# Cached memory keys turned in 32x32 squares on VectorE, their scores as 32x32 products on sixteen tiles of the array, and the pools laid out anew

## The chip, the cores and the metric

The kernel runs on one core of a Trainium2 chip. The time is device time in microseconds (us) of one launch; the time before is the median of 3 runs. The engines are named PE (TensorE matmuls; PEld is its weight load), DVE (VectorE), ACT (ScalarE), POOL (GpSimd) and SP (SyncE, which issues most of the DMAs). Each engine works through its own instructions in a fixed order, so an instruction that waits holds all that stand behind it on that engine.

## The reference

One layer of a hybrid decoder serves a prompt group of 512 rows and a sample group of 8 sequences with 4 new tokens each (32 rows), with the same weights, all in f32. The mixer (an mLSTM and a differential attention) comes first, cross-attention second, a ConvFFN last. The change lies in the cross-attention:

```python
def mem_attend(h, mk, mv, w_mq, w_mo):
    B, T, _ = h.shape
    q = (h @ w_mq).reshape(B, T, MEM_HEADS, MEM_HEAD_DIM)
    s = jnp.einsum('bqhd,bkhd->bhqk', q.astype(jnp.float32), mk.astype(jnp.float32)) * (MEM_HEAD_DIM ** -0.5)
    p = jax.nn.softmax(s, axis=-1)
    o = jnp.einsum('bhqk,bkhd->bqhd', p, mv.astype(jnp.float32)).reshape(B, T, D_MODEL)
    return o.astype(h.dtype) @ w_mo
...
yp, ... = layer(yp, pos_p, da_attend_prompt, ..., mk_p, mv_p, ...)        # keys and values from mem_prompt
ys, ... = layer(ys, pos_s, attend_s, ..., cache_mem_k[l], cache_mem_v[l], ...)
```

There are 4 heads of 256 and 256 memory tokens. The prompt attends to one memory whose keys and values the kernel computes itself. Each sample sequence attends to a memory of its own that is cached in DRAM: keys and values of 256 tokens x 1024 numbers each, 1 MB and 1 MB for one sequence, 8 MB and 8 MB in all.

## The kernel before

Rows lie on 128 partitions. A product of two f32 matrices is made of three with numbers of reduced mantissa (a high part and a rest, "split": ACT casts, DVE subtracts); a matmul whose operands stay f32 leaves two records in the trace (the samples' scores and value products are of this kind).

*Weights.* Class `Weights` holds a plan. A slot (`slot_tile`, pool `wp`, tag "W", `NSLOT` = 4 buffers) holds 512 KB of a weight matrix, split; a stage (`stage`, pool `stg`, 6 buffers of 4 KB a partition) takes what the DMA brings. `pump` emits the loads for as many slots as are free, `get` hands one out in turn and `free` gives it back.

*The cross-attention* is written in this order. `mem_v` computes the prompt memory's values; the prompt memory's own keys and values are read back from DRAM (`mk_d`, `mv_d`) and split into `mkT` and `mvN`. Then comes the query projection, called the q gemm below: `gemmB` over 8 column blocks m of `w_mq`, 48 matmuls each. The first four run with `half_first=True` (all blocks of one half of the columns before the other, L465), the others block by block (L477). `ev_q` splits each result into `qh` and `ql`, and copies the samples' 32 columns into `qs`.

*The samples' keys.* `mk_load(i)` brings half a sequence's keys into a stage (16 loads of 512 KB), tokens on partitions. `mk_turn(i)` turns it by eight PE transposes (L1416, PSUM tile `tpk`) and two copies, one on ACT and one on DVE (L1417), into `kT`, which uses a weight slot. `mk_scores(b)` multiplies one sequence (L1424, `ssc`): for each head two matmuls, 128 rows of contraction x 32 queries, all 32 sample rows against that sequence's 256 keys; `sample_exp` takes the maximum and the exponential from PSUM.

*The prompt's softmax* is a pipeline `prompt` of 8 steps, of which `next(prompt)` emits one: `ch_soft` (scores `sca`, maximum `cnm` on DVE, exponential `cp` on ACT, reciprocal `csu`, scaling of `cp` on DVE), `ch_turn` (transposes `cpt`, split into `pT`), `ch_out` (products `cpo` with the values, split into `oT`). `mv_load(b)` brings a sequence's values into two stages `wst`, or into a weight slot as `vt`, and `mv_out(b)` multiplies (`pso`). `ost` turns its result. Then the output projection with `w_mo` begins (L407 to L409, `mm<-wslot,oT`).

*What sets the order.* A list scheduler puts the instructions of each engine in an order, starting from the order in which they are written; `tc.issue_after(x)` keeps the instructions written under it behind x, `burst` holds a run of matmuls together. A tile of a pool can be written again only when all that read its buffer before are done. The order around the change:

```python
    for i in range(6):
        mk_load(i)
    for i, _ in enumerate(gemmB(hqT, [ev_q(m) for m in range(4, 8)])):
        if i % 4 == 3:
            for j in (i // 2 - 1, i // 2):
                mk_turn(j)
                mk_load(j + 6)
```

so that keys are loaded six halves ahead of their transposes. Then come one step of `prompt`, the scores of sequences 0 to 3, the transposes of sequences 4 to 7 with a step between, the first value loads, a step, the other scores, more value loads, and the rest of the steps.

## Time and profile before

| | |
|---|---|
| median of 3 runs | 960.0 us (959.2 to 962.14) |
| profiled execution | 957.37 us, its span 955.6 us, mean granted clock 0.994 |
| PE busy | 933.3 us, 6619 matmuls |
| DVE, ACT, POOL busy | 600.3, 387.7, 196.4 us |
| q gemm | starts at 381.78 us, last matmuls at 435.80 us |
| `w_mo` projection | starts at 491.42 us |
| PE records of L1416 (`tpk`) | 128, 16.5 us of busy time |
| PE records of L1424 (`ssc`) | 128, 7.9 us of busy time |

A line of a group reads: source line, engine, operation, output<-inputs by the program's names, tile rows*columns on PE, shape and count, then busy time, mean ns of one, and the idle time of the engine just before these instructions with what ended it. A line of a timeline begins with start and length in us. Matmuls overlap in the pipeline, so the distance of two starts is a better price than a length.

### The profile page before, as it was taken

What the parts mean: (1) busy time and instruction counts of PE and PEld (TensorE: products, weight loads), DVE (VectorE), ACT (ScalarE), POOL (GpSimd) and SP (SyncE); (2) the same over time, 40 slices, a digit from 0 to 9 for tenths busy, and PEclk for the clock granted to TensorE, in tenths of its full rate; (3) what the DMA queues carried; (4) which work ended last, traced back from release to release, by engine and by line L of the source; (5) the groups of instructions that cost most, each with busy time, mean ns of one, the idle gap of its engine ahead of it and who ended that gap; (6) DMA issues with size and microseconds to landing.
All of it is one profiled execution on the core that took longest, in us unless ns stands there. A gap on an engine that the chain in (4) does not pass through costs nothing. (4 is left out here: it accounts for less than half of the span.)

```text
span 955.6 us, 17087 instructions
## 1 busy us (share of the span) xinstructions
PE 933.3 (98%) x6619; PEld 810.2 (85%) x6619; DVE 600.3 (63%) x1129; ACT 387.7 (41%) x750; POOL 196.4 (21%) x383
## 2 busy tenths in 40 slices
PE   8999999999999999999999999999999999999995
PEld 5899787889766778998767799989988997999974
DVE  6745145565886448635654769727758676676767
ACT  5655134344676357635544523332212222222232
POOL 6610000115432216300000454001110110110114
PEclk9999999999999999999999999999999999999998
DMA  8950023344825539946954743063053313512023
GB/s 296 296 178 1 1 88 136 88 131 137 275 82 171 173 100 346 289 137 188 344 195 115 206 133 88 4 177 89 4 144 82 119 26 81 162 48 89 24 92 116
DMA packets 120674, 130.27 MB, mean 136 GB/s; under 512 B 8568, under 2 KB 86233, under 8 KB 120593
## 3 DMA queue, kind: packets, MB, share of 16 engines
q1 hardware_dynamic: 114408, 125.69, 42.3%
q10 hardware_dynamic: 6184, 3.48, 1.2%
q8 instruction: 52, 0.85, 0.4%
q14 instruction: 30, 0.24, 0.1%
HBM read 112.22 MB, written 16.93 MB: 135 GB/s over the span
## 5 line engine op out<-in xcount | busy, mean ns | idle before, releaser
L146 ACT CAST wslot<-wst 128x1024 fp32r<-128x1024 f32 x125 | 130.8, 1050 | 261.3 <-issue 73.5
L477 PE MATMUL mm<-fT,wslot 128*128 128x256 f32 x1872 | 235.9, 288 | 0.0
L477 PEld LDWEIGHTS mm<-fT,wslot 128*128 128x128 f32 x1872 | 234.4, 188 | 1.8 <-issue 0.8
L147 DVE TENSOR_TENSOR wslot<-wst,wslot 128x1024 fp32r<-128x1024 f32 x125 | 154.4, 1238 | 91.8 <-ACT wslot L146 91.4
L1689 PE MATMUL mm<-wslot,act 128*128 128x512 f32 (+1 forms) x180 | 70.2, 391 | 0.0
L1690 PE MATMUL mm<-wslot,act 128*128 128x512 f32 (+1 forms) x180 | 70.0, 392 | 0.0
L1688 PE MATMUL mm<-wslot,act 128*128 128x512 f32 (+1 forms) x180 | 69.3, 387 | 0.0
L1596 POOL COPY cvo<-u 128x2 f32<-128x2 f32 x43 | 11.0, 256 | 204.7 <-DVE u L1594 194.6
L407 PE MATMUL mm<-wslot,hT 128*128 128x512 f32 x128 | 51.6, 403 | 0.0
L477 PE MATMUL mm<-hT,wslot 128*128 128x256 f32 (+1 forms) x384 | 51.0, 289 | 0.0
L409 PE MATMUL mm<-wslot,hT 128*128 128x512 f32 x128 | 51.0, 400 | 0.0
L408 PE MATMUL mm<-wslot,hT 128*128 128x512 f32 x128 | 50.7, 396 | 0.0
L1591 DVE TENSOR_TENSOR u<-mm,rsb 128x256 f32<-128x256 f32 x43 | 18.2, 424 | 51.0 <-PE mm L477 50.0
L477 PEld LDWEIGHTS mm<-hT,wslot 128*128 128x128 f32 x384 | 49.2, 188 | 0.5 <-issue 0.2
L1688 PEld LDWEIGHTS mm<-wslot,act 128*128 128x128 f32 x180 | 34.3, 191 | 8.0 <-issue 0.4
L1690 PEld LDWEIGHTS mm<-wslot,act 128*128 128x128 f32 x180 | 33.8, 188 | 7.2 <-issue 0.4
L1689 PEld LDWEIGHTS mm<-wslot,act 128*128 128x128 f32 x180 | 33.8, 188 | 7.2
L1608 ACT ACTIVATE c<-c 128x560 f32<-128x560 f32 x21 | 14.1, 672 | 56.5 <-DVE c L1602 56.5
L1602 DVE SCALAR_TENSOR_TENSOR c<-u,cvT,c 128x560 f32<-128x560 f32 x43 | 34.3, 798 | 0.9
L1601 DVE SCALAR_TENSOR_TENSOR c<-u,cvT,c 128x560 f32<-128x560 f32 x43 | 34.1, 793 | 0.2
L1701 DVE TENSOR_TENSOR yp<-mm,yp 128x512 f32<-128x512 f32 (+1 forms) x41 | 27.2, 674 | 5.1 <-PE mm L1690 5.0
L409 PEld LDWEIGHTS mm<-wslot,hT 128*128 128x128 f32 x128 | 24.1, 188 | 5.1
(474 smaller groups left out, 1863.8 us busy)
## 6 DMA issues: line engine op xcount, KB each, us to landing
wst<-in_w_up_dram SPq DMA_DIRECT2D x42, 512.0 KB
wst<-in_w_in_dram SPq DMA_DIRECT2D x28, 512.0 KB
wst<-in_w_down_dram SPq DMA_DIRECT2D x20, 512.0 KB
wst<-in_cache_mem_k_dram SPq DMA_DIRECT2D x16, 512.0 KB
wst<-in_w_mk_dram SPq DMA_DIRECT2D x8, 512.0 KB
xb<-in_x_prompt_dram SPq DMA_DIRECT2D x8, 512.0 KB
wst<-in_cache_dk_dram SPq DMA_DIRECT2D x16, 256.0 KB
wst<-in_cache_dv_dram SPq DMA_DIRECT2D x16, 256.0 KB
```

Source lines behind the costliest of these rows:

```text
L146: nc.scalar.copy(out=hi, in_=src)
L147: (eng or nc.vector).tensor_tensor(out=lo, in0=src, in1=f32(hi), op=SUB)
L407: mm(ps[b], lhsT=xt.hi(k, c0, c0 + n), rhs=s[:, 0, kk, :], start=(k == 0), stop=False)
L408: mm(ps[b], lhsT=xt.hi(k, c0, c0 + n), rhs=s[:, 1, kk, :], start=False, stop=False)
L409: return mm(ps[b], lhsT=xt.lo(k, c0, c0 + n), rhs=s[:, 0, kk, :], start=False, stop=(k == nk - 1))
L477: mm(ps[i], lhsT=s[:, l, k, :], rhs=x(k, c0, c1), start=(k == 0 and j == 0), stop=(k == 7 and j == 2))
L1601: STT(out=c, in0=u[:, 1:EXT - 1], scalar=w[1], in1=c, op0=MUL, op1=ADD)
L1602: STT(out=c, in0=u[:, 0:EXT - 2], scalar=w[0], in1=c, op0=MUL, op1=ADD)
L1688: mm(ps, lhsT=t[:, 0, c0:c0 + P], rhs=s[:, 0, i % 2, cs], start=st, stop=False)
L1689: mm(ps, lhsT=t[:, 0, c0:c0 + P], rhs=s[:, 1, i % 2, cs], start=False, stop=False)
L1690: return mm(ps, lhsT=t[:, 1, c0:c0 + P], rhs=s[:, 0, i % 2, cs], start=False, stop=en)
L1701: VTT(out=y, in0=ps, in1=y, op=ADD)
```

## The change

- The samples' keys of four sequences come straight into one tile `kq` (32 KB a partition, pool "k" with one buffer). `mk_turn(b)` turns each half of a sequence in place with one DVE instruction that transposes every 32x32 square of 128x1024. `tpk`, its copies and `kT` go.
- `q_spread` copies `qs` into `qrep`, such that each group of 32 partitions holds what each other one holds; 16 copies per half, on POOL, ACT and DVE in turn.
- `mk_scores(g)` works on four sequences at once: 128 matmuls of 32 rows of contraction x 32 queries x 256 columns, over 4 row groups and 4 column groups of the array, into 4 PSUM banks; four copies put the sums in order, then one maximum and four exponentials.
- The pools of weights and stages can be closed and opened again at other places. For the q gemm there are 2 slots and 2 stages in place of 4 and 6; stages are 6 again behind it, slots 4 again behind the second scores. All of `w_mq` now goes through the block-by-block form.
- The reads of `mk_d` and `mv_d` move into the q gemm (`own_memory`), and so do the 24 small loads of `cr` for the convolution, which move from SP's queue to ACT's (`conv_rows`).

```diff
-    for m in range(8):
-        slotB(w_mq, [(P * m, P)])
...
+    closed("st")
+    closed("w")
+    opened("w", 2, "left")
+    opened("st", 2, "left")
+    opened("k", 1, "right")
+    W.nslots = 2
+    for m in range(8):
+        slotB(w_mq, [(P * m, P)])
+    W.pump()
...
+            nc.scalar.dma_start(out=cr[p0 + q0:p0 + q0 + m, o:o + n], in_=src[:, c0:c0 + n])
...
-    run(gemmB(hqT, [ev_q(m) for m in range(4)], half_first=True))
...
+    def mk_load(b):
+        if b % 4 == 0:
+            kts[b // 4] = lay["k"][1].tile([P, 4, 2, DM], F32, name="kq", tag="K")
         for c in range(2):
-            for h in range(H):
-                t = mm(ps[NS * h:NS * h + NS], lhsT=qs[:, 2 * h + c], rhs=kts[b][:, 2 * h + c, :], start=(c == 0), stop=(c == 1))
-        sample_exp(sall, b, ps, nm, su)
-        return t.ins
+            dma(out=kts[b // 4][:, b % 4, c], in_=I["cache_mem_k"][0, b, c * P:(c + 1) * P].rearrange("t h d -> t (h d)"))
+
+    def mk_turn(b):
+        for c in range(2):
+            k = kts[b // 4][:, b % 4, c]
+            nc.vector.transpose(k, k)
+
+    def q_spread(m0):
+        n = 0
+        for j in range(4):
+            for i in range(4):
+                e = (nc.gpsimd.tensor_copy, nc.scalar.copy, VCP)[n % 3]
+                n += 1
+                e(out=qrep[NS * i:NS * i + NS, m0:m0 + 4, j, :], in_=qs[NS * j:NS * j + NS, m0:m0 + 4, :])
+
+    def mk_scores(g):
+        ps = [mmp("ssc") for _ in range(4)]
+        kt = kts[g].rearrange("p b c (j r) -> p (b c) j r", r=NS)
+        t = None
+        for j in range(8):
+            for i in range(4):
+                r = slice(NS * i, NS * i + NS)
+                for h in range(H):
+                    with burst(t):
+                        t = mm(ps[i][NS * h:NS * h + NS, :256], lhsT=qrep[r, 2 * h + j // 4, j % 4, :], rhs=kt[r, :, 8 * h + j, :],
+                               start=(j == 0), stop=(j == 7)).ins
...
+    mk_load(0)
+    for i, _ in enumerate(gemmB(hqT, [ev_q(m) for m in range(8)])):
         if i % 4 == 3:
-            for j in (i // 2 - 1, i // 2):
-                mk_turn(j)
-                mk_load(j + 6)
+            m = i // 4
+            if m < 4:
+                if m < 3:
+
+                    with tc.issue_after(wdma[-1].ins):
+                        mk_load(m + 1)
+                own_memory(m)
+                conv_rows(2 * m)
+                conv_rows(2 * m + 1)
+            if 1 < m < 6:
+                mk_turn(m - 2)
+            if m % 4 == 3:
+                q_spread(m - 3)
+    closed("st")
+    closed("w")
+    opened("st", 6, "left")
...
+    mk_scores(0)
+    mv_load(0)
+    mv_load(1)
+    for b in range(4, NB):
+        mk_load(b)
+    mv_load(2)
     next(prompt)
+    for b in range(4, NB):
+        mk_turn(b)
+    for _ in range(3):
+        next(prompt)
+    mk_scores(1)
+    closed("k")
+    opened("w", NSLOT, "right")
```

What the scheduler makes of it on DVE, around the softmax of the prompt's first steps and the keys of sequences 4 to 7. Before (`kT<-tpk` copies turned keys out of PSUM, `cnm`, `csu`, `cp` and `pT` are the prompt's softmax):

```order
L1035 TENSOR_REDUCE snm<-ssc 128x1 x2
L1417 COPY kT<-tpk 128x4x128
L1370 TENSOR_REDUCE cnm<-sca 128x2
L147 TENSOR_TENSOR pT<-cpt,pT 128x256
L1417 COPY kT<-tpk 128x4x128
L1374 RECIPROCAL csu<-csu 128x2
L1376 TENSOR_SCALAR cp<-cp,csu 128x256
L1417 COPY kT<-tpk 128x4x128
L1376 TENSOR_SCALAR cp<-cp,csu 128x256
L147 TENSOR_TENSOR pT<-cpt,pT 128x256
```

and now, on DVE from the maximum of the first score group on:

```order
L1470 TENSOR_REDUCE snm<-cas 128x4
L1445 STREAM_TRANSPOSE kq<-kq 128x1024
L1399 TENSOR_REDUCE cnm<-sca 128x2
L1445 STREAM_TRANSPOSE kq<-kq 128x1024
L157 TENSOR_TENSOR pT<-cpt,pT 128x256
L1403 RECIPROCAL csu<-csu 128x2
L1445 STREAM_TRANSPOSE kq<-kq 128x1024
L1399 TENSOR_REDUCE cnm<-sca 128x2
L1405 TENSOR_SCALAR cp<-cp,csu 128x256 x2
L157 TENSOR_TENSOR pT<-cpt,pT 128x256
L1445 STREAM_TRANSPOSE kq<-kq 128x1024 x2
```

Where copies out of PSUM stood, transposes of the loaded tile stand, and the first is ahead of the softmax's maximum.

On SP's queue, the loads around the q gemm's end. Before (`cr` are the convolution's rows, `xb<-x_d` the residual rows read back):

```order
L1407 DMA wst<-in_cache_mem_k_dram 128x1024
L1510 DMA cr<-in_w_dw_dram 3x64
L1511 DMA cr<-in_b_dw_dram 1x64
L1509 DMA cr<-in_state_conv_dram 16x64
L1510 DMA cr<-in_w_dw_dram 3x64
L1511 DMA cr<-in_b_dw_dram 1x64
L1407 DMA wst<-in_cache_mem_k_dram 128x1024
L1119 DMA xb<-x_d_2549 32x1024
L1407 DMA wst<-in_cache_mem_k_dram 128x1024
L1436 DMA wst<-in_cache_mem_v_dram 128x1024 x6
L1436 DMA vt<-in_cache_mem_v_dram 128x1024 x8
```

and now, on SP's queue from the fourth block of the weights on:

```order
L266 DMA wst<-in_w_mq_dram 128x8x128
L1440 DMA kq<-in_cache_mem_k_dram 128x1024 x2
L1349 DMA wst<-mk_d 128x1024
L266 DMA wst<-in_w_mq_dram 128x8x128
L1440 DMA kq<-in_cache_mem_k_dram 128x1024 x2
L1353 DMA wst<-mv_d 128x1024
L266 DMA wst<-in_w_mq_dram 128x8x128
L1353 DMA wst<-mv_d 128x1024
L266 DMA wst<-in_w_mq_dram 128x8x128 x2
L1483 DMA wst<-in_cache_mem_v_dram 128x1024 x6
L1440 DMA kq<-in_cache_mem_k_dram 128x1024 x8
L1131 DMA xb<-x_d_2549 32x1024
```

The keys of sequences 4 to 7 stood ahead of all values, one by one; they now stand as a block of eight behind six loads of values, and weights, keys and the own memory take turns ahead of that.

On PE, at the second half of the scores. Before (`tpk` are the keys' transposes):

```order
L1367 MATMUL sca<-mkT,qh 128x256 x2
L1367 MATMUL sca<-mkT,ql 128x256
L1416 MATMUL tpk<-cpk,wst 128x128 x40
L1424 MATMUL ssc<-kT,qs 32x256 x32
L1385 MATMUL cpt<-cpk,cp 128x128 x4
```

and now, on PE:

```order
L1396 MATMUL sca<-mkT,qh 128x256 x2
L1396 MATMUL sca<-mkT,ql 128x256
L1426 MATMUL cpo<-pT,mvN 128x512 x10
L1464 MATMUL ssc<-kq,qrep 32x256 x128
L1414 MATMUL cpt<-cpk,cp 128x128 x4
```

The transposes, which needed no result of the softmax, are gone from between its steps; what is left there depends on DVE and ACT.

More of the change, by code (lines that the diff above doesn't have):

```diff
@@ L209, in stage @@
     def stage():
-        return stg.tile([P, 1024], F32, name="wst", tag="st")
+        return lay["st"][1].tile([P, 1024], F32, name="wst", tag="st")
     def slot_tile():
-        return wp.tile([P, 2, 1024], F32R, name="wslot", tag="W")
+        return lay["w"][1].tile([P, 2, 1024], F32R, name="wslot", tag="W")
     def split_w(sv, st, share):
@@ L243, in slotsA @@
             slotA(w, k, n0, share=share)
+    wdma = []
     def slotB(w, ranges, share=False, extra=False):
@@ L1400, in ch_out @@
             put(oT, h // 2, j, j + 1, 0, SEQ, po.unsqueeze(1))
-    kst, kts, vts = {}, {}, {}
-    def mk_load(i):
-        b, c = i // 2, i % 2
-        kst[i] = stage()
-        dma(out=kst[i], in_=I["cache_mem_k"][0, b, c * P:(c + 1) * P].rearrange("t h d -> t (h d)"))
-    def mk_turn(i):
-        b, c = i // 2, i % 2
-        if c == 0:
-            kts[b] = wp.tile([P, 8, 256], F32, name="kT", tag="W")
-        for q in range(2):
-            ps = at("tpk")
-            for j in range(4):
-                t = tr(ps[:, j * P:(j + 1) * P], kst[i][:, (4 * q + j) * P:(4 * q + j + 1) * P], ident)
-            (VCP if q else nc.scalar.copy)(out=kts[b][:, 4 * q:4 * q + 4, c * P:(c + 1) * P], in_=v2(ps, P))
-        return t.ins
@@ new lines, in mk_turn @@
+    def mk_turn(b):
[20 more added lines that the diff above has]
+                               start=(j == 0), stop=(j == 7)).ins
+        b4 = slice(4 * g, 4 * g + 4)
+        for i in range(4):
+            (VCP if i % 2 else nc.scalar.copy)(out=sall[:, b4, :].rearrange("p b (c i r) -> p b c i r", c=2, i=4)[:, :, :, i, :],
+                                               in_=ps[i][:, :256].rearrange("p (b c r) -> p b c r", c=2, r=NS))
+        VRED(out=nm[:, b4], in_=sall[:, b4, :], axis=AX.X, op=MAX, negate=True)
+        for b in range(4 * g, 4 * g + 4):
+            ACT(out=sall[:, b, :], in_=sall[:, b, :], func=AF.Exp, bias=nm[:, b:b + 1], accum_out=su[:, b:b + 1])
+        return t
```

71 lines of the change are left out of this document (28 added, 43 removed).

## The prediction

> **What bounds the kernel now.** I read the head of the page first, then the timeline of TensorE (PE) from the query projection (the q gemm) to the output projection, then the groups of VectorE (DVE), ScalarE (ACT), SyncE's queue (SP), and the table by stretches.
>
> ```profile
> span 955.6 us, 17087 instructions
> PE 933.3 (98%) x6619; PEld 810.2 (85%) x6619; DVE 600.3 (63%) x1129; ACT 387.7 (41%) x750; POOL 196.4 (21%) x383
> ```
>
> PE is busy 98% of the span; no other engine is near it. Work taken off PE should shorten the kernel, as long as PE doesn't begin to wait. This is the part that the change touches (start, length, line, out<-in, tile, count; a length holds the last matmul's tail, so I take pitches from start to start):
>
> ```profile
> 412.91 1.47 PE L1416 MATMUL tpk<-cpk,wst 128*128 128x128 f32 x12
> 414.13 2.51 PE L477 MATMUL mm<-hqT,wslot 128*128 128x256 f32 x18
> 416.48 0.60 PE L1416 MATMUL tpk<-cpk,wst 128*128 128x128 f32 x4
> 416.83 4.00 PE L477 MATMUL mm<-hqT,wslot 128*128 128x256 f32 x30
> 436.19 1.03 PE L1416 MATMUL tpk<-cpk,wst 128*128 128x128 f32 x8
> 437.41 0.48 PE L1367 MATMUL sca<-mkT,qh 128*128 128x256 f32 x2
> 439.00 1.05 PE L1424 MATMUL ssc<-kT,qs 128*32 128x256 f32 x10
> 439.99 0.65 PE L1416 MATMUL tpk<-cpk,wst 128*128 128x128 f32 x4
> 440.57 3.22 PE L1424 MATMUL ssc<-kT,qs 128*32 128x256 f32 x54
> 443.72 1.53 PE L1416 MATMUL tpk<-cpk,wst 128*128 128x128 f32 x12
> 445.01 0.48 PE L1367 MATMUL sca<-mkT,qh 128*128 128x256 f32 x2
> 449.68 5.09 PE L1416 MATMUL tpk<-cpk,wst 128*128 128x128 f32 x40
> 454.70 3.66 PE L1424 MATMUL ssc<-kT,qs 128*32 128x256 f32 x64
> 458.29 0.66 PE L1385 MATMUL cpt<-cpk,cp 128*128 128x128 f32 x4
> 489.94 0.44 PE L1497 MATMUL ost<-cpk,oS 128*128 128x128 f32 x2 [1.50 <-ACT oS L1494]
> 490.86 0.72 PE L1397 MATMUL cpo<-pT,mvN 128*128 128x512 f32 x2
> 491.42 0.39 PE L407 MATMUL mm<-wslot,oT 128*128 128x512 f32 x1
> ```
>
> One wait stands in it, 1.50 us before `ost`. The prompt's softmax (`sca`, `cpt`, `cpo`) is mixed with transposes and scores, so PE has independent work while DVE and ACT finish a softmax; the DMA has room at first and little later (columns: us, busy time of PE, PEld, DVE, ACT, POOL with counts, clock, DMA share, GB/s):
>
> ```profile
> 440.00:450.00 10.00, 10.00 (x114) 8.38 (x114) 6.55 (x17) 6.15 (x21) 0.00 (x0) 1.00 0.55 154
> 460.00:470.00 10.00, 10.00 (x75) 8.23 (x74) 7.05 (x19) 6.46 (x28) 0.00 (x0) 1.00 1.03 408
> 520.00:525.00 5.00, 5.00 (x31) 3.80 (x21) 2.79 (x6) 2.72 (x5) 0.00 (x0) 1.00 1.11 294
> ```
>
> **PE work removed.** A block of 16 transposes within the q gemm takes 1.22 us (412.91 to 414.13) and 0.35 (416.48 to 416.83). Three such blocks, 4.71 us, lie before 436.19. Behind that: 1.22 (436.19 to 437.41), 0.58, 1.29, the block of 40 with 5.02, and 12 among `sca` at about 0.1 each, 1.14. All transposes: 13.96. The scores take 0.99 + 3.15 + 3.59 = 7.73. Together 21.7 us.
>
> **PE work added.** 256 products of 32x32 tiles, each two records, so 512 records with 256 columns. The shape is not in the trace; the bounds are. 54 score records with a 128x32 tile take 3.15 us, 58 ns each, with four column tiles in turn; a tile is therefore held about 233 ns. If all sixteen tiles work side by side, a record costs 15 ns and all cost 7.5 us, the lower end. If a row of tiles excludes the others, the price is 58 ns, 30 us, the upper end. How fast small products can be issued at all shows here:
>
> ```profile
> 229.98 0.25 PE L958 MATMUL mlg<-nT,qT 128*32 128x8 f32 x8
> 230.06 1.93 PE L962 MATMUL mlsi<-wst,qzm 128*32 128x128 f32 x64
> ```
>
> Eight records left in 0.08 us, 10 ns each, and the 64 behind them at about 29 ns with tiles held half as long, so issue is not the limit at 15. I take 7.5, 3.75 per group of four sequences. The Trainium skill ("TensorE: Matmul & The Clock Gate", section "Wait — 56ns, not 53.3ns?") says that starts are never closer than about 25 ns; 512 of them would be 12.8 us, an estimate from that page, and 5.3 us more than the sum here. The 10 ns row speaks against it for separate tiles.
>
> If nothing waited, PE would gain 21.7 - 7.5 = 14.2 us, and the 1.50 before `ost` as well, since `ost` now stands behind output-projection matmuls: 15.7 us, or 944. The question is how much PE waits.
>
> **First wait: the q gemm's weights.** One column block m of it takes 6.1 us (2.51 and 4.00 less tails, 48 records). Before, four slots and six stages were filled ahead. Now there are two of each, and the stages also carry the memory's own keys and values. From m = 3 on, a weight load can be issued only when the split of the block before has freed its stage. Such a load, and the split:
>
> ```profile
> 518.35 11.16 SPq L254 DMA_DIRECT2D wst<-in_w_up_dram  x8
> 522.52 1.05 ACT L146 CAST wslot<-wst 128x1024 fp32r<-128x1024 f32 x1 [1.64 <-DMA wst<-in_w_up_dram]
> 523.60 1.23 DVE L147 TENSOR_TENSOR wslot<-wst,wslot 128x1024 fp32r<-128x1024 f32 x1 [2.15 <-ACT wslot L146]
> ```
>
> Issue to cast 4.17, cast 1.05, subtraction 1.23: 6.5 us against 6.1 for a block, and more where a 512 KB key transfer is ahead in the queue (1.3 us at 408 GB/s) or a transpose ahead on DVE. The chain has four such links and some 2 us of slack at its start. Ends: 0 (all in the slack) and 8 (two key transfers ahead in each link, less slack). I take 3. ACT also gets the 24 small conv loads, 0.3 us each by SP's row, 7 us in all; they can hold a cast when their issue waits, which is in the 3.
>
> ```profile
> 425.71 0.30 SPq L1510 DMA_DIRECT2D cr<-in_w_dw_dram  x1
> L1064 ACT COPY caz<-spt 128x32 f32<-128x32 f32 x8 | 0.8, 223 | 0.0
> L1417 ACT COPY kT<-tpk 128x512 f32<-128x512 f32 x16 | 9.4, 588 | 2.6 <-PE tpk L1416 2.4
> ```
>
> **The end of the q gemm**, called E, would be 436.19 - 4.71 = 431.5 without the wait. Behind it come 12 `sca` (437.41 to 439.00, 1.6 us); the spread of the queries, 16 copies on three engines behind the last evacuation, keeps the first score waiting about 1.3 us (five small copies of 0.22 us on an engine, and an evacuation); the scores end at E + 6.6.
>
> **Second wait: the second group's keys.** This is the heart of the forecast. There is one key tile for four sequences, so the second group's loads start only when the first group's last score is done. On SP's queue they stand behind six value loads, which wait for the end of the q gemm.
>
> ```profile
> wst<-in_cache_mem_k_dram SPq DMA_DIRECT2D x16, 512.0 KB
> 448.81 6.32 SPq L1436 DMA_DIRECT2D wst<-in_cache_mem_v_dram  x6
> 455.94 5.49 SPq L1436 DMA_DIRECT2D vt<-in_cache_mem_v_dram  x8
> ```
>
> At 408 GB/s each 512 KB needs 1.28 us. Six value loads fill the DMA to about E + 8.5; eight key loads land from E + 10.5 to E + 19.5. On DVE the eight transposes of this group stand in turn with the prompt's softmax, the first ahead of the softmax's next maximum. So the softmax waits for transfers too. The DVE work there, by rows:
>
> ```profile
> L147 DVE TENSOR_TENSOR wslot<-wst,wslot 128x1024 fp32r<-128x1024 f32 x8 | 9.7, 1223 | 11.1 <-ACT wslot L146 11.1
> L1417 DVE COPY kT<-tpk 128x512 f32<-128x512 f32 x16 | 11.0, 687 | 9.1 <-PE tpk L1416 9.1
> L1370 DVE TENSOR_REDUCE cnm<-sca 128x2 f32<-128x512 f32 x8 | 5.5, 690 | 3.7 <-PE sca L1367 3.6
> L147 DVE TENSOR_TENSOR pT<-cpt,pT 128x256 fp32r<-128x256 f32 x16 | 6.7, 421 | 4.1 <-ACT pT L146 3.9
> L1376 DVE TENSOR_SCALAR cp<-cp,csu 128x256 f32<-128x256 f32 x16 | 5.1, 350 | 0.2
> ```
>
> A transpose of 128x1024 isn't in the trace. The subtraction of that size (1223 ns) is nearest; two 128x512 copies from PSUM are 1374. Ends 1.1 and 2.4 (twice the subtraction); I take 1.2. Between the first and the last transpose stand three maxima (2.1), three `pT` (1.3), four scalings (1.4) and two reciprocals (0.3): with eight transposes 14.7 us from E + 10.5, so to E + 25, and two more `pT` and the `cpo` behind them bring the second scores to E + 27.5. PE's own work up to there is 1.6 + 1.3 + 3.75 and 48 `sca`, 12 `cpt`, 12 `cpo` (9.9 us at about 0.12, 0.1 and 0.23 each), 16.5. PE so waits about 11 us here, where it waited nothing. Ends: 4 (values and keys pass side by side and transposes at 1.1) and 20 (transposes at 2.4).
>
> **Behind the second scores** (3.75 us) the value tiles `vt` take the keys' place: eight loads, 10.3 us, against some 13 us of PE work ahead of the first `pso`; hidden. A last softmax that has lost its cover costs about 1 us (0 to 3).
>
> **At no cost:** 16 DVE and 16 ACT copies of keys go (11.0 us and 9.4 at 588 ns), both engines having room; the evacuation copies and one maximum per group replace eight maxima and lie beside PE work; the conv loads leave SP's queue.
>
> **Sum:** 15.7 gained, less 3 + 1.3 + 11 + 1 = 16.3 waited: 0.6 us slower. The profiled execution took 957.37 us (span 955.6 and 1.77 around it), so 958.0 there; against the median of 960.0, the same step gives 960.6, and I say 960.5. From no change a measurement here can tell about 0.3%, 2.9 us.
>
> **Rivals.** (a) The waits are short: q gemm fed in time, PE covering much of the key transfer. For it: PE has `sca` and `cpo` to do, and DVE and ACT are under 75% busy in all rows. Against it: the order on DVE puts each softmax step behind a transpose. With the low ends (0 + 1.3 + 4) the gain is 10.4, 949.6; with no wait at all 944.3. (b) The sixteen tiles don't run side by side, or issue binds at 25 to 29 ns: at 29 ns, 14.8 us of scores, 7.3 more, 968; the sign is decided from about 20 ns on. For it: no row here has four rows of tiles in use. Against it: the 10 ns row. If instead rows of tiles take turns, 30 us of scores and 983. By the Trainium skill's 25 ns it would be 966. (c) Transposes at 2.4 us: 8 x 1.2 more on DVE's chain, 970; decided from 1.6 us on. (d) The q gemm starves, 8 us in place of 3: 965.5; decided from 6. For it: 6.5 against 6.1 with nothing in front. That the products stay whole and the change does nothing can't be; the instructions are others.
>
> **Chances.** The case of the sum 0.47: its waits move it by some 4 us to either side (956 to 965), so of it 0.13 faster, 0.24 the same, 0.10 slower. (a) 0.23, nearly all faster. (b) 0.10 (issue 0.07, rows in turn 0.03), (c) 0.10 and (d) 0.10, slower but for 0.05 that other terms make up. So faster 0.36, same 0.29, slower 0.35. The range reaches from (a) with its low ends, less a little, to (b): 947 to 968.
>
> **What would show it.** Right: no `tpk` of keys, score records at about 15 ns from start to start, and PE idle about 11 us between the two score groups, released by DVE, whose own idle time is put down to the `kq` transfers. Wrong: score groups of over 5 us; transposes far from 1.2 us; PE idle in the q gemm by more than 5 us or not at all; or PE busy through the second group's load, which would leave the gain whole.

## The result: 1.4% slower

After the change the median is 972.55 us (968.41 to 975.15, 4 runs) against 959.6 of before on the same chip (957.26 to 962.14, 4 runs): 1.0136 times, interval 1.0113 to 1.016. The forecast was 960.5, with 947 to 968 as its range. The profiled execution has a span of 968.9 us; before it was 955.6. The head of the page after:

```profile
span 968.9 us, 17576 instructions
PE 933.1 (96%) x6875; PEld 804.3 (83%) x6875; DVE 612.9 (63%) x1137; ACT 383.6 (40%) x748; POOL 200.2 (21%) x395
```

PE is busy as long as before (933.3), though 21.7 us of its work went and the new products take less: other work came back as longer busy time (why, the last section says), and the span grew by waits. PE's timeline of after, where before had its list (start, length, line, out<-in, tile, count, and in brackets the idle time before a row and what ended it):

```profile
439.82 0.39 PE L1396 MATMUL sca<-mkT,qh 128*128 128x256 f32 x2
...
441.32 3.41 PE L1464 MATMUL ssc<-kq,qrep 32*32 32x256 f32 x116
445.36 1.46 PE L1464 MATMUL ssc<-kq,qrep 32*32 32x256 f32 x60 [0.63 <-DVE qrep L1453]
448.65 2.92 PE L1464 MATMUL ssc<-kq,qrep 32*32 32x256 f32 x80 [1.83 <-issue]
451.50 0.80 PE L1396 MATMUL sca<-mkT,qh 128*128 128x256 f32 x2
...
460.83 0.44 PE L1414 MATMUL cpt<-cpk,cp 128*128 128x128 f32 x1 [3.78 <-DVE cp L1405]
...
464.94 1.22 PE L1426 MATMUL cpo<-pT,mvN 128*128 128x512 f32 x2 [0.46 <-ACT pT L156]
...
468.05 0.50 PE L1396 MATMUL sca<-mkT,qh 128*128 128x256 f32 x2 [1.39 <-ACT cp L1402]
...
471.98 0.76 PE L1464 MATMUL ssc<-kq,qrep 32*32 32x256 f32 x24
473.16 4.28 PE L1464 MATMUL ssc<-kq,qrep 32*32 32x256 f32 x205 [0.42 <-DVE oT L157]
478.47 0.71 PE L1464 MATMUL ssc<-kq,qrep 32*32 32x256 f32 x27 [1.03 <-issue]
479.11 0.66 PE L1414 MATMUL cpt<-cpk,cp 128*128 128x128 f32 x4
...
505.60 0.50 PE L419 MATMUL mm<-wslot,oT 128*128 128x512 f32 x1
...
511.02 0.38 PE L1554 MATMUL ost<-cpk,oS 128*128 128x128 f32 x2
```

The transposes are gone, and `ost` no longer holds PE. But the score groups last from 441.32 to 451.50 and from 471.98 to 479.11, 10.18 and 7.14 us, where 3.75 each was forecast. Within them PE stands still for 0.63, 1.83, 0.42 and 1.03 us, twice with "issue" as the reason: nothing that the profile shows held it. Between them it stands still for 5.63 us (3.78, 0.46 and 1.39). From these starts the touched part divides into stretches (us; the q gemm from its first matmul; "first scores" from its end to the end of the first score group; "behind" up to the first output-projection matmul, where the forecast is what its sum leaves):

| | q gemm | first scores | between | second scores | behind |
|---|---|---|---|---|---|
| forecast | 52.7 | 6.65 | 20.9 | 3.75 | 26.2 |
| after | 57.06 | 11.68 | 20.48 | 7.14 | 26.48 |
| difference | +4.4 | +5.0 | -0.4 | +3.4 | +0.2 |

They add to 12.6 us; the profiled execution took 970.69, 12.7 more than the 958.0 forecast for it. So two terms failed, the projection's wait and the price of the score groups, and the large one, the wait between the groups, came out as forecast. That a size is right doesn't yet make its reason right.

### The profile page after: what moved, and what is told of

Its sections match the earlier page's. It is cut to its first block, busy times and chain, and to the rows that moved or that the text cites. A ratio compares the mean times of both kernels' runs of the same rounds, so it can differ in the third digit from the quotient of the medians.

```text
span 968.9 us, 17576 instructions
## 1 busy us (share of the span) xinstructions
PE 933.1 (96%) x6875; PEld 804.3 (83%) x6875; DVE 612.9 (63%) x1137; ACT 383.6 (40%) x748; POOL 200.2 (21%) x395
## 4 chain that ended last, share of the span: by engine, by line
PE 75%; DVE 9%; DMA 6%; ACT 4%; issue 2%; POOL 2%; SPq 0%; DVEq 0%; ACTq 0%; POOLq 0%
PE mm L489 31%; PE mm L419 5%; PE mm L420 5%; PE mm L421 5%; PE mm L477 4%; PE mm L1733 4%; PE mm L1731 4%; PE mm L1732 4%; DVE wslot L157 1%; DMA xb<-in_x_prompt_dram 1%; PE mm L398 1%; DVE xb L1146 1%; PE sda L1223 1%; DMA kq<-in_cache_mem_k_dram 1%; ACT wslot L156 1%
## 5 line engine op out<-in xcount | busy, mean ns | idle before, releaser
L489 PE MATMUL mm<-hqT,wslot 128*128 128x256 f32 (+1 forms) x384 | 51.6, 295 | 5.2 <-ACT wslot L156 4.2
L489 PEld LDWEIGHTS mm<-hqT,wslot 128*128 128x128 f32 x384 | 50.3, 194 | 6.2 <-ACT wslot L156 4.7
```

The costliest lines, as they stand in the source:

```text
L489: mm(ps[i], lhsT=s[:, l, k, :], rhs=x(k, c0, c1), start=(k == 0 and j == 0), stop=(k == 7 and j == 2))
```

## The experiments

All on the two theories that the table leaves. A: a 32x32 record costs more than 15 ns, and PE's pauses add to it. B: with two slots and two stages the projection starves; rival to B: it is the conv loads' issue on ACT's queue. For the wait between the groups: transfer or transposes. All were timed in turn with the kernel before, in groups on four chips, whose medians for the kernel before are 958.03 to 959.42, so ratios and stretches compare better than medians. Stretches as above (in e7 and e8 some of the prompt's `sca` stand ahead of the projection's last block and count in it); the q gemm starts at 382.4 to 386.3 us, which the edits don't set.

| | q gemm | first scores | between | second | median us | ratio to before, 95% |
|---|---|---|---|---|---|---|
| e1_conv_sp | 54.11 | 11.69 | 21.93 | 8.17 | 970.5 | 1.0113 (1.0096 to 1.013) |
| e2_reuse | 56.56 | 10.56 | 13.13 | 6.33 | 963.4 | 1.0043 (1.0024 to 1.0062) |
| e3_n128 | 58.52 | 10.68 | 18.83 | 5.99 | 969.43 | 1.0089 (1.0064 to 1.0113) |
| e4_keys_first | 58.28 | 8.70 | 20.18 | 6.68 | 969.56 | 1.0098 (1.0072 to 1.0125) |
| e5_conv_late_keys_first | 53.34 | 8.69 | 19.37 | 8.29 | 963.92 | 1.0062 (1.004 to 1.0084) |
| e6_reuse_conv_sp | 54.50 | 11.40 | 13.63 | 7.01 | 960.06 | 1.0024 (0.9998 to 1.005) |
| e7_turns_held | 55.35 | 10.36 | 17.36 | 10.07 | 967.4 | 1.0102 (1.0077 to 1.0126) |
| e8_half | 56.42 | 12.93 | 11.79 | 3.59 | 972.3 | 1.0144 (1.0118 to 1.0171) |
| e9_softmax_ahead | 53.50 | 8.70 | 23.69 | 7.32 | 967.5 | 1.0091 (1.0069 to 1.0112) |
| e10_one_j | 53.13 | 5.95 | 18.91 | 1.79 | 956.62 | 0.9973 (0.9956 to 0.999) |
| e11_rows_inner | 53.00 | 8.70 | 19.82 | 6.78 | 965.05 | 1.0059 (1.004 to 1.0078) |
| e12_turns_no_load | 52.73 | 11.15 | 18.41 | 7.17 | 965.45 | 1.0069 (1.0044 to 1.0093) |
| e13_no_keys | 59.14 | 12.28 | 13.64 | 6.65 | 966.72 | 1.0078 (1.0048 to 1.0108) |

### The projection: e1_conv_sp

In the timeline of after, ACT (ACTq: its DMA issues) shows a cast that waited:

```profile
386.88 0.38 ACT L1378 ACTIVATE qh<-mm 128x256 fp32r<-128x256 f32 x1
...
390.22 0.34 ACTq L1367 DMA_DIRECT2D cr<-in_state_conv_dram  x1
...
395.72 0.23 ACTq L1367 DMA_DIRECT2D cr<-in_b_dw_dram  x1
...
397.95 1.04 ACT L156 CAST wslot<-wst 128x1024 fp32r<-128x1024 f32 x1 [10.69 <-DMA cr<-in_w_dw_dram]
```

ACT did no arithmetic for 10.69 us: it stood in the conv loads' issue, and the next weights' cast stood behind them. On PE of after:

```profile
384.73 11.32 PE L489 MATMUL mm<-hqT,wslot 128*128 128x256 f32 x86
399.05 0.76 PE L489 MATMUL mm<-hqT,wslot 128*128 128x256 f32 x4 [3.00 <-ACT wslot L156]
...
420.89 0.76 PE L489 MATMUL mm<-hqT,wslot 128*128 128x256 f32 x4 [1.23 <-ACT wslot L156]
```

The edit sends these loads through SP, behind the projection:

```diff
-            nc.scalar.dma_start(out=cr[...], in_=src[...])
+            dma(out=cr[...], in_=src[...])
@@ in the projection's loop
-                conv_rows(2 * m)
-                conv_rows(2 * m + 1)
@@ behind it
+    for g in range(8):
+        conv_rows(g)
```

> The 24 small conv loads go back to SP's queue, behind the weights of the query projection, as before the change; nothing else differs. Theory A (the query projection starved because ACT stood behind conv loads that waited for landings: 10.7 us between two of ACT's instructions from 386.9 to 398.0 in the changed kernel): the waits of 3.0 and 0.5 us in front of the third block go, and the low clock behind them; the projection ends 4 to 6 us earlier and the kernel takes 966 to 969 against 972.6. Theory B (two slots and two stages starve it, whoever issues the conv loads): waits of about the same sum remain, at most 1 us is gained, 971 to 973.

The q gemm fell by 2.95 us to 54.11, and the cast that waited 10.69 us starts at 392.76, 5.2 us earlier. So the rival to B takes 3 of the 4.4 us that the projection is over its forecast; theory A had 4 to 6 us, theory B at most 1. What is left is mostly a wait on DVE's half of the split. In the timelines of e1_conv_sp, first PE's, then SP's:

```profile
399.19 12.45 PE L489 MATMUL mm<-hqT,wslot 128*128 128x256 f32 x96 [2.13 <-DVE wslot L157]
```

```profile
450.58 0.32 SPq L1367 DMA_DIRECT2D cr<-in_state_conv_dram  x1
451.63 3.96 SPq L1440 DMA_DIRECT2D kq<-in_cache_mem_k_dram  x8
```

Little of the gain reached the end (970.5, where theory A had 966 to 969): the conv loads now stood ahead of the second group's key loads on SP, which left at 451.63 though the first scores had ended at 449.02, and the wait between the groups grew by 1.45 us.

### The second group's keys taken away: e2_reuse, e6_reuse_conv_sp

```diff
-    for b in range(4, NB):
-        mk_load(b)
+    kts[1] = kts[0]
...
-    for b in range(4, NB):
-        mk_turn(b)
```

> The keys of sequences 4 to 7 are neither loaded nor turned; the second scores use the first group's keys, so those sequences' scores are not the reference's. Theory A (the wait for the second group's keys costs about what was forecast, 10 to 11 us between the two score groups): PE has 20.5 us there in the changed kernel and only 10 of work, so the stretch shrinks to 10 to 13 us and the kernel takes 962 to 965. Theory B (the softmax of the prompt itself is the bound there, now that no transposes of keys cover it): the stretch stays above 17 us and less than 4 us are gained, 969 to 972.

The stretch between the groups fell from 20.48 to 13.13 us, and the median by 9.1, theory A. It is the largest single term. The 13.13 that stay hold 9.9 us of PE work by the prediction's count; in e2's PE timeline they are 10.6 of work and two waits of the softmax itself:

```profile
455.46 0.30 PE L1414 MATMUL cpt<-cpk,cp 128*128 128x128 f32 x1 [2.09 <-DVE cp L1405]
...
457.97 0.73 PE L1426 MATMUL cpo<-pT,mvN 128*128 128x512 f32 x2 [0.46 <-ACT pT L156]
```

With both edits:

> Both at once: the second group's keys neither loaded nor turned (its scores use the first group's keys and are not the reference's), and the conv loads on SP's queue. Theory A (the two causes are independent; without the second wait the 2.7 us at the query projection reach the end): 960 to 961.5, 2 to 3.4 us under the run without the second keys. Theory B (ACT's queue behind the conv loads is worth nothing in the end): 963 to 964.

The median lies in theory A's range, but the two runs were on different chips. By the ratios e6 gains some 1.8 us over e2, with intervals that overlap, and in the profiled executions nothing: the four stretches add to 86.5 us in e6 and 86.6 in e2, since the three behind the projection took back its 2.1. That the two costs are independent is so not shown. Even without the second group's keys and with the projection's gain the kernel only meets the one before, 1.0024.

### The records' price: e3_n128, e11_rows_inner, e10_one_j

e3_n128 leaves the products' number and shortens them to half the columns:

```diff
-  ...mm(ps[i][NS*h:NS*h+NS, :256], ..., rhs=kt[r, :, 8*h+j, :],
+  ...mm(ps[i][NS*h:NS*h+NS, :128], ..., rhs=kt[r, 0:4, 8*h+j, :],
```

> Score products over 128 columns in place of 256 (half of the keys; the other half of the scores is a copy of the first), with the same number of matmuls and weight loads; the evacuation has eight smaller copies per group in place of four. Theory A (a score record is priced by what PE has to issue and fetch, not by the array): the second group's records stay near 20 ns from start to start and its 7.1 us at 6.5 to 7.5, pauses of over 1 us included; the kernel takes 971 to 973. Theory B (the array's tiles are the bound, 14.6 ns at 256 columns): the pitch falls to about 8 ns, the second group to 3 to 4 us, the kernel to 965 to 968.

Its second score group in PE's timeline:

```profile
474.78 2.90 PE L1464 MATMUL ssc<-kq,qrep 32*32 32x128 f32 x205 [0.95 <-DVE oT L157]
478.92 0.50 PE L1464 MATMUL ssc<-kq,qrep 32*32 32x128 f32 x27 [1.24 <-issue]
```

A row's length ends with its last record's own, 0.29 us here and 0.37 with 256 columns. The starts of the 205 records so lie within 2.61 us, 12.8 ns apart, against 3.91, 19.1 ns, with 256 columns: neither theory A's 20 nor theory B's 8, and the time, 969.43, is between the two as well. Half the columns saves 6.4 ns, so a record of 256 is some 12.7 ns of columns, near the 15 taken, and 6.4 that don't go with the columns. Times sixteen tiles that is about 103 ns for each use of a tile. The weight loads of after have that length (count, then least, median and longest ns; the records' own lengths in after and then in e3 below):

```profile
L1464 PEld LDWEIGHTS ssc<-kq,qrep x512: 101/104/172, 441.3 to 478.6; 32*32 32x32 f32 x171
L1464 PE MATMUL ssc<-kq,qrep x512: 371/396/629, 441.3 to 478.8; 32*32 32x256 f32 x171
```

```profile
L1464 PE MATMUL ssc<-kq,qrep x512: 264/290/418, 445.4 to 479.2; 32*32 32x128 f32 x171
```

So a tile seems to be held for its load (104) and its columns (about 203), and the forecast took the columns alone. The fixed share is measured; that it is the load is an inference from equal lengths. The starts in the traces leave it open: they come in batches of 34 records, most of them 16 to 17 ns apart in after, with a gap of about 160 ns behind each batch (42 to 45 in e3), where two rounds of sixteen tiles would be 32.

The Trainium skill ("TensorE: Matmul & The Clock Gate", Part 3, section "The mechanism") says that a weight load overlaps running matmuls only if its row group differs. In the kernel four products in a row, eight records, share theirs. e11_rows_inner, built on e5, changes the row group with each product:

```diff
-            for i in range(4):
-                r = slice(NS * i, NS * i + NS)
-                for h in range(H):
+            for h in range(H):
+                for i in range(4):
+                    r = slice(NS * i, NS * i + NS)
```

> As the run with late conv loads and keys first, with the loops of the score products exchanged: the four row groups of the array inside, the four column groups (heads) outside. Theory A (a pass holds its tile for the matmul and its weight load, 216 + about 125 ns, whatever the order): pitch 20 to 22 ns, 963 to 965. Theory B (the order keeps weight loads from going ahead): 15 to 17 ns, 1 to 2 us less per group, 960 to 962.

Its PE timeline:

```profile
467.68 4.84 PE L1464 MATMUL ssc<-kq,qrep 32*32 32x256 f32 x226 [0.39 <-DVE oT L157]
472.81 0.70 PE L1464 MATMUL ssc<-kq,qrep 32*32 32x256 f32 x26 [0.29 <-issue]
```

The starts lie within 4.84 - 0.37 = 4.47 us, 19.9 ns a record: no gain, theory A. A batch of 34 takes 647 ns in both orders, so the order of the tiles is not what keeps the fixed share visible. The Trainium skill's floor of about 25 ns between starts (the same title, section "Wait — 56ns, not 53.3ns?"), weighed in the prediction, is contradicted for separate tiles by the 19.1 and 12.8 ns.

e10_one_j, also built on e5, keeps one product in eight, and with it nearly all else:

```diff
-        for j in range(8):
+        for j in range(1):
```

> As the run with late conv loads and keys first, with one of the eight products of each score left in (64 score records in place of 512), so the samples' scores are not the reference's; loads, transposes, copies and softmax stay. Theory A (the score products cost about 21 ns a record and the pauses behind fetched code, 7.2 and 8.3 us in that run, all of it on the path): each group falls to 1 to 2.5 us, its wait for the queries' copies included; 11 to 12.5 us less, 951.5 to 954. Theory B (the second keys' transfer is the path, and time won at the first scores is waited for later; the clock falls again): 6 to 8 us, 956 to 958.

First scores 5.95 and second 1.79, 9.2 us less than e5 in these stretches; 956.62 is in theory B's range, and 0.9973 times before against e5's 1.0062 is some 8.5 us. With almost no score products left the new layout, in e5's order, would gain 0.3% (0.1 to 0.4). That is the bound of what a cheaper product could bring.

### PE's pauses: e4_keys_first, e5_conv_late_keys_first

Value loads wait until the second group's keys are issued; e5_conv_late_keys_first does it with the conv loads too:

```diff
+    with tc.issue_after(kdma[-1].ins):
+        for b in range(3):
+            mv_load(b)
```

> On SP's queue the eight loads of the second group's keys stand ahead of the first six loads of values, not behind; nothing else differs. In the changed kernel the keys were issued at 451.6, just after the first scores, when six value loads had mostly been moved (440.0 to about 450). Theory A (the place in the queue counts little, since the keys wait for the first scores anyway): the second scores begin at most 2 us earlier; but the values come later, up to 3 us are lost at the value products or nothing: 971 to 974. Theory B (the values delay the keys as the prediction's sum has it, E + 8.5 against E + 6.6): 2 us or more are gained, 968 to 971.

> The conv loads are on SP's queue again, but behind the second group's keys (where they stood in the run with the conv loads alone they delayed these keys: the first scores were done at 449.0, the keys issued from 451.6); and these keys stand ahead of the values. Theory A (the two losses add: about 2.7 us at the end of the query projection, 3 us between the start of the first scores and the start of the second): 965.5 to 968. Theory B (whatever is won ahead is lost in the wait for the second keys, which has its own length, as in the run with the conv loads alone): 969 to 971.

The first score group fell to 7.19 us in both, from 10.18. PE's timeline of e5 shows why:

```profile
438.22 3.41 PE L1464 MATMUL ssc<-kq,qrep 32*32 32x256 f32 x116
442.26 3.22 PE L1464 MATMUL ssc<-kq,qrep 32*32 32x256 f32 x140 [0.63 <-DVE qrep L1453]
...
455.03 0.45 PE L1414 MATMUL cpt<-cpk,cp 128*128 128x128 f32 x1 [6.04 <-DVE cp L1405]
```

No "issue" pause. In after, a transfer on the queue of instructions begins at 446.40, 5.1 us after the first score record, and takes 0.89 us while six value loads fill the data queue; PE goes on 2.25 us after its start. In e4 and e5 the data queue is nearly empty during the first scores, such a transfer begins 2.2 and 2.3 us after the first record, and the pause is gone; e4 differs from after in the order of these loads alone. 512 records of small products are many instructions in little time, and that PE outran their supply fits the pause of the second group too: a transfer begins at 476.15, and PE goes on at 478.47, 2.32 us later. But the data queue was idle then (a DMA share of 0.03), so a full queue is not the only way to such a pause.

e4 came out in theory B's range, 969.56, but by the pause, 3.0 us of the first scores, and not by earlier keys: the stretch between the groups is 0.3 us shorter. e5, 963.92, is better than both its theories. Its four stretches add to 6.7 us less than those of after: 3.7 in the projection, 3.0 in the first scores and 1.1 between, less 1.2 in the second scores, part of which ran at a granted clock of 0.50 (467.7 to 471.1). What the earlier transposes save is partly waited out: 6.04 us for `cp`, since the prompt's softmax stands behind them on DVE. e5 and e11_rows_inner on top of it are the best kernels with the whole computation that were run; at 1.0062 and 1.0059 times before they are still slower.

The 0.63 ahead of the second group of rows has another reason. The queries' copies (DVE) and a clearing on POOL in the timeline of after:

```profile
442.15 3.16 DVE L1453 COPY qrep<-qs 32x128 f32<-32x128 f32 x5
```

```profile
443.43 1.80 POOL L1062 MEMSET caz<- 128x2048 f32 x1
```

Five copies take 3.16 us together, where the median of all ten on DVE is 240 ns, and the longest takes 1.83, as long as POOL's clearing of a 128x2048 tile (1.80) beside it. In e7, where that clearing ran earlier and POOL copied no queries, no copy on DVE took more than 0.22. The Trainium skill ("SBUF — State Buffer", section "SBUF: two separate sides") says that DVE, in some of its operations, and GpSimd share a pair of ports which one of them holds for a whole instruction; the trace agrees, 1.83 against 1.80 us.

### What the wait between the groups consists of: e12_turns_no_load, e9_softmax_ahead

e12_turns_no_load is e6 with the second group's transposes, done on the first group's keys, and no load. On DVE each pair of them stands behind a scaling of the softmax, so their order is not that of after:

```diff
+    kts[1] = kts[0]
+    mv_load(2)
     for b in range(4, NB):
-        mk_load(b)
...
+        with tc.issue_after(scl[-1].ins):
+            mk_turn(b)
         next(prompt)
```

> As the run with the first group's keys used twice and conv loads on SP (960.1, 13.6 us between the score groups), but the eight transposes of the second group stay on DVE, two between each two softmax steps; they turn the first group's keys once more, so there is still no second transfer and the scores are not the reference's. Theory A (the transfer makes the second wait; the transposes, 9.8 us, fit into DVE's idle time): the stretch is 13.5 to 16 us, 960 to 962.5. Theory B (the transposes on DVE between the softmax steps make it, transfer or not): 17.5 to 20 us, 963.5 to 966.

18.41 us between the groups against 13.63 without the transposes (e6) and 19.37 to 20.48 with load (e5, after). So the transposes are worth 4.8 us, theory B, and the transfer 1 to 2, as far as the other order allows the comparison. In the PE timeline of e12_turns_no_load the scores wait for them with nothing to load:

```profile
468.05 7.24 PE L1464 MATMUL ssc<-kq,qrep 32*32 32x256 f32 x256 [2.55 <-DVE kq L1445]
```

The prediction gave the wait to the transfer and the transposes in turn. The size was right; the transfer was not the larger part. The transposes of both groups in after, and then three rows of its DVE timeline between the score groups:

```profile
L1445 DVE STREAM_TRANSPOSE kq<-kq 128x1024 f32<-128x1024 f32 x16 | 19.6, 1231 | 8.6 <-DMA kq<-in_cache_mem_k_dram 8.6
```

```profile
455.36 1.25 DVE L1445 STREAM_TRANSPOSE kq<-kq 128x1024 f32<-128x1024 f32 x1 [1.99 <-DMA kq<-in_cache_mem_k_dram]
...
467.23 1.22 DVE L1445 STREAM_TRANSPOSE kq<-kq 128x1024 f32<-128x1024 f32 x1
...
469.92 0.68 DVE L1399 TENSOR_REDUCE cnm<-sca 128x2 f32<-128x512 f32 x1
```

1.23 us for a transpose, 1.2 forecast. DVE waits for a key once, 1.99 us, and from 455.36 to 470.6 it has no gap: behind the first landing it is DVE's own work that holds PE up. Since the softmax stood behind the transposes on DVE, e9_softmax_ahead put it ahead, on top of e5:

```diff
+    next(prompt)
+    for b in (4, 5):
+        with tc.issue_after(scl[-1].ins):
             mk_turn(b)
```

> As the run with late conv loads and keys first (963.9), but on DVE the second group's transposes stand behind the softmax steps written before them: two steps, four transposes, a step, two transposes, a step, two transposes. Theory A (the prompt's softmax idles because it stands behind transposes that wait for their keys: DVE idle while PE waited 6.0 us for a scaling in that run): the 6.0 us wait shrinks to 2 or less, the stretch between the two score groups from 19.4 to 15 to 17 us, 960 to 962.5. Theory B (transfer and transposes alone set the stretch, 10.3 us for eight loads and one transpose behind): 18.5 to 20 us, 963 to 964.5.

A miss for both theories: 967.5, and the four stretches add to 3.5 us more than e5's. The wait for the softmax fell from 6.0 to 2.7 us, but PE then waited 2.73 us for a `pT` behind the transposes and 4.36 for the keys themselves, in its timeline:

```profile
469.82 7.39 PE L1464 MATMUL ssc<-kq,qrep 32*32 32x256 f32 x256 [4.36 <-DVE kq L1445]
```

Both chains need DVE, and PE needs both; in the orders that were run, one or the other of them is late.

### Other covers: e7_turns_held, e8_half, e13_no_keys

e7_turns_held, on top of e5, holds the first group's transposes back behind the queries' split, and spreads the queries on ACT and DVE alone:

```diff
+                with tc.issue_after(evl[-1].ins):
                     mk_turn(m - 2)
-                e = (nc.gpsimd.tensor_copy, nc.scalar.copy, VCP)[n % 3]
+                e = (nc.scalar.copy, VCP)[n % 2]
```

> As the run with late conv loads and keys first, and two more edits: the first group's transposes on DVE are held behind the split of the projection block written before them, so that no split of weights waits behind a transpose that waits for its keys (2.1 us of PE idle, released by DVE, at 399.2 in the run with the conv loads alone); and the queries are spread by ACT and DVE alone, since five DVE copies took 3.16 us while POOL copied at the same time, 0.63 us each, as against 0.2 elsewhere. Theory A (these two waits are real): the projection's stretch falls to 50.5 to 52.5 us, the first scores start at most 1 us later than their operands allow, another 2 to 4 us: 962 to 965. Theory B (two slots set the pace of the projection, and the spread's wait is ACT's): less than 1 us.

Outside both theories, and 3.5 us worse than e5 on the same chip. The wait for DVE's split near 399 is gone, but PE waited for ACT's casts instead, 0.59 and 1.28 us, and the projection took 55.35; the first scores took 10.36 us in place of e5's 8.69, and the second group 10.07. PE's timeline:

```profile
441.27 0.98 PE L1464 MATMUL ssc<-kq,qrep 32*32 32x256 f32 x32 [1.72 <-ACT qrep L1453]
```

The queries' copies are late on two engines. e8_half, on top of e7, takes the old way for the second four sequences (stages, PE transposes, 128x32 scores) and the new one for the first:

```diff
+    def o_turn(i):
...
+                t = tr(ps[:, j * P:(j + 1) * P], ost[i][:, (4 * q + j) * P:(4 * q + j + 1) * P], ident)
...
+    def o_scores(b):
...
+                t = mm(ps[NS * h:NS * h + NS], lhsT=qs[:, 2 * h + c], rhs=kts[b][:, 2 * h + c, :], start=(c == 0), stop=(c == 1))
```

> As the run before it for sequences 0 to 3; the keys of sequences 4 to 7 are treated as before the change: six halves loaded into stages from the end of the query projection, turned by 64 PE transposes and two copies each, scored with 128x32 tiles. Theory A (the change loses because the second group's transfer and transposes have no independent PE work beside them; PE transposes in that place are cover): no idle stretch on PE behind the first scores, the second scores start about 15 us behind the first, and of the 21.7 us of removed work half is saved: 954 to 960. Theory B (the new scores and the projection with two slots cost more than they save by themselves): 961 to 966.

No gain, 972.3, outside both theories. PE's timeline:

```profile
443.84 5.25 PE L1464 MATMUL ssc<-kq,qrep 32*32 32x256 f32 x173 [1.73 <-ACT qrep L1453]
450.93 2.88 PE L1464 MATMUL ssc<-kq,qrep 32*32 32x256 f32 x79 [1.83 <-issue]
...
503.68 0.69 PE L1583 MATMUL ost<-cpk,oS 128*128 128x128 f32 x2 [4.42 <-ACT oS L1580]
```

The cover between the groups came back: the second scores start 11.79 us behind the first, with one wait of 0.27. Its worth was spent on the projection (56.42 us), on the first scores (12.93) and behind, where PE waits 4.42 us before `ost` and the granted clock is 0.50 from 502.6 for 6.8 us. As e7's two edits are in it, it does not price the old way alone.

e13_no_keys takes the key loads out of the projection, to leave the two slots and stages alone with the weights; in place of transposes DVE clears the tiles:

```diff
-            nc.vector.transpose(k, k)
+            nc.vector.memset(k, 0.0)
```

> As the run with the first group's keys used twice and conv loads on SP, but the first group's keys are neither loaded nor turned: DVE fills the tile with zeros (eight memsets) ahead of the projection, and the scores are not the reference's. In the projection only the weights, with two slots and two stages, and the own memory are left. Theory A (keys in the queue and transposes ahead of weight splits starve the projection): it takes 49.5 to 51 us in place of 54.5. Theory B (a load, a cast and a subtraction with two slots and two stages take longer than a block): 52.5 to 54.5 us still.

Its time as a whole tells little: the clearings stood ahead of the projection's own input on DVE and cost PE 7.82 us. Behind that wait its PE timeline has one row for 360 records:

```profile
395.18 47.61 PE L489 MATMUL mm<-hqT,wslot 128*128 128x288 f32 x360 [7.82 <-ACT hqT L156]
```

No wait in it, and 59.14 less the 7.82 is 51.3. Two slots and two stages feed the projection once the conv loads are off ACT's queue and the cached keys' loads and transposes are out of the way, which speaks for theory A. It does not settle it: PE's late start let the weights run ahead, and loads and transposes went together, so which of them held the projection up is not shown.

## Why the prediction was wrong

**The score groups** (3.75 us each, behind a wait of 1.3): the step that failed first. The groups took 10.18 and 7.14 us, 9.8 more than the 7.5 of the sum. Of this, 2.3 are the price of a record: 512 records at 19.1 ns are 9.8 us. The column time was right, 12.7 by the difference of two sizes; the 6.4 ns a record that don't go with the columns were missing. Bounding a 32x32 record by a sixteenth of a tile's hold, as seen with four tiles in use, left them out. The other 7.5 us are time in which the records don't follow each other at this pace, for which the sum had nothing inside a group: 2.86 us idle for "issue", 0.63 for the queries' copies and 0.42 for DVE's `oT`, and some 3.6 that count as busy, namely the last records' own length ahead of each of the four waits, the first 20 records, 35 ns apart, and the last 80 of the first group, 29.0 ns apart at a granted clock of 0.50 for the most part (20.3 in e2, where the clock stayed at 1.00). Rival (b) was decided from 20 ns on, with a chance of 0.10. At 19.1 ns the record stays short of it, and its mechanism (issue binds at 25 to 29 ns) is not what the runs showed; a pause in the supply of instructions was in neither the sum nor the rivals.

**The projection** (3 us of 0 to 8): 7.4 measured, 57.06 less the 49.7 without a wait. That is rival (d), and its price of 8. The prediction named ACT's conv loads and counted them as 0.3 us of issue each, within the 3. ACT stood 10.69 us among them, far longer than the issue rows last. e1 puts 3 us of the 7.4 on them. For the rest e1 shows waits on DVE's half of the split, with the key transposes on the same engine; that they are the cause is argued, and e7, which held them back, gained nothing. A part is the clock (below).

**The wait between the groups** (11): right in size, 20.5 us against 20.9 for the stretch, and on DVE in kind as well. The forecast had the first transpose 3.9 us behind the end of the first scores and 14.7 us of DVE work from there; measured are 3.86 (451.50 to 455.36) and 15.2 without a gap. Of the 10.6 us that the stretch exceeds PE's work, some 3.5 are the softmax without cover (13.13 to 13.63 in e2 and e6), 4.8 the transposes and 1 to 2 the transfer. What it had wrong is what PE does meanwhile: its sign was 11 us of idle time, and PE idled for 5.63. The rest was PE's own work, largely at half the clock, 14.85 us for what took 10.6 in e2 (the sum had 9.9, a little low, and its own pitches give 9.7). That these two add to the 11 that were forecast is luck.

**Right as put:** transposes at 1.2 us (1.23), so rival (c) falls; value tiles hidden; `ost` at no cost (511.02 is behind output-projection matmuls); the stretch behind (26.48 against 26.2, a wait of some 1.2 where 1 was forecast). Rival (a), the waits short, falls by e2: the second group's keys alone are worth 9.1 us.

The ledger by stretches: 23.2 us removed (21.7 and 1.5); records 9.8, the rest of the score groups 7.5, projection 7.4, between the groups 10.6 and behind 1.2 added, 36.5. The 13.3 more are the distance between the spans, 968.9 and 955.6.

## What to carry to other kernels

Price a small-tile product by what goes with its columns and what doesn't, and find both from two sizes. Where a change takes cheap filler work off the bound engine, count what that filler was hiding: here 21.7 us of transposes and scores on PE were the cover of a softmax and of a transfer, and most of them came back as waits. A DMA issued on a computing engine's queue can hold that engine for far longer than its issue lasts, here 10.69 us with eight issues of 0.2 to 0.3 us in it. And where a wait was forecast, look at what the engine did in it: here half of it was work at a low clock.

## What was not expected of the hardware

The granted clock fell behind some of PE's waits. The table by stretches of after (us, busy time of PE, PEld, DVE, ACT, POOL with counts, clock, DMA share, GB/s):

```profile
445.00:450.00 5.00, 2.81 (x125) 1.80 (x126) 1.09 (x4) 0.00 (x0) 0.23 (x1) 0.91 0.93 365
450.00:455.00 5.00, 5.00 (x62) 4.07 (x32) 2.07 (x3) 2.33 (x9) 0.00 (x0) 0.50 0.49 152
460.00:465.00 5.00, 3.71 (x17) 3.34 (x17) 5.00 (x10) 1.40 (x5) 0.00 (x0) 0.50 0.92 349
```

and of e2:

```profile
450.00:455.00 5.00, 3.36 (x28) 3.16 (x28) 2.40 (x5) 3.47 (x14) 0.00 (x0) 1.00 0.07 27
```

In the touched part of after the granted clock is 0.50 from 401.3 for 3.4 us (behind the projection's wait of 3.00), from 449.1 for 6.8 (behind the pause of 1.83) and from 459.3 for 6.8 (behind the wait for `cp`); three `sca` records start 0.64 us apart there and 0.35 at full clock. Not every wait did it: in e2 a pause of 1.63 us at the same place left the clock at 1.00. A wait can so cost a second time, in the work behind it. In the projection that is at most half of 3.4 us, and in the first scores the last 80 records show it. Between the groups DVE had no gap, so whether the low clock made that stretch longer, or only filled PE's waiting, is not shown. The mean clock is 0.985, where before it was 0.994.
